# A hybrid decoder step: the RWKV-7 mixer with paired VectorE products, output masks of both head halves at once, and small matmuls on 128 rows

## The chip, the cores and the metric

The kernel runs on one core of a Trainium2 chip. The metric is the device time of one execution in microseconds (us). A core has TensorE (PE, with its weight loads shown apart as PEld), VectorE (DVE), ScalarE (ACT), GpSimd (POOL) and SyncE (SP), which issues most DMAs here. Each engine works through its own instructions in order and waits on semaphores for the others.

## The reference, cut to what matters

One inference step of two layers: layer 0 is a Conformer convolution, layer 1 is RWKV-7 time mixing, and each is followed by a squared-ReLU MLP (1024 → 4096 → 1024). There is one prompt of 1024 tokens behind 16 meta tokens, and 8 samples of one token. Everything is float32. The change lies in layer 1's mixer (16 heads of 64):

```python
def _wkv7_step(S, inp):
    r_t, w_t, k_t, v_t, kk_t, a_t = inp
    sa = jnp.einsum('bhvk,bhk->bhv', S, -kk_t)
    S = (S * w_t[:, :, None, :] + sa[..., None] * (kk_t * a_t)[:, :, None, :]
         + v_t[..., None] * k_t[:, :, None, :])
    y = jnp.einsum('bhvk,bhk->bhv', S, r_t)
    return S, y
...
    r = (xr @ w_r); k = (xk @ w_k); v = (xv @ w_v)
    w_log = -jax.nn.softplus(-(w0 + jnp.tanh(xw @ w1) @ w2)) - 0.5
    decay = jnp.exp(-jnp.exp(w_log))
    a = jax.nn.sigmoid(a0 + (xa @ a1) @ a2)
    g = jax.nn.sigmoid(xg @ g1) @ g2
    kk = k * k_k;  kk = kk / max(|kk| over the head, 1e-12)
    k = k * (1.0 + (a - 1.0) * k_a)
    S_final, ys = lax.scan(_wkv7_step, S0, ...)       # over 1040 tokens
    yn = groupnorm(y per head) * gn_g + gn_b
    out = ((yn + bonus(r, k, v)) * g) @ w_o
```

## The kernel before, in words

A float32 product is made of two half-precise parts, a high and a low one ("hi", "lo", of the type fp32r), and `mm3` (L188 to L190) issues three matmuls for each product: hi·hi, hi·lo, lo·hi. Raw weights come by DMA (`wv_raw`), ACT rounds them to the high part (L158) and DVE or POOL subtracts to get the low part (L163). Activations go the same way (`mx` → `mh`, `ml`, L141 and L142).

The whole step is one function, `hybrid_step`, written as Python generators that are woven into each other; a scheduler then fixes one static order of instructions per engine from its own cost model. Each engine keeps that order. Tiles come from pools with a fixed number of buffers under a tag, so that a tile waits until the last reader of the tile that had its buffer before has finished.

The time runs like this in the profiled execution: layer 0 until about 1105 us; then layer 1's mixers, and behind them the layer-1 MLP until the end. The mixers take the tokens in four groups, g = 0 to 3 (272 columns in group 0: 256 prompt tokens and 16 meta tokens; 256 or 264 in the others). For each group (`mixer_in`) an r loop, a k loop and a v loop run over p = 0 to 7, p being a block of 128 features, two heads. In the k loop, the squares of k are summed per head (`pn`), and `norms` makes the reciprocal norms `r16`, as a hi and a lo part. In the v loop, for each p:

- `l_w` and `l_a` (`lora2`) are the decay's and the rate's low-rank products. Their left sides lie in one tile, `lwah`/`lwal`, w in rows 0 to 63 and a in rows 64 to 127, so that each matmul contracts 64 rows. ACT makes `wa` of both (tanh, then one Copy over both halves).
- `pb` spreads `r16` from heads to features (`spread`, L710), contracting 32 rows.
- DVE makes `kk`, the running sum of the decay (`cum`, by a scan, L1022), `bb` = kk·a, `km`, and four products `ab` (L1050 to L1053) against exponentials `ex` and `em` from ACT.
- `vt` is the transposed v, which ACT copies from PSUM and SP stores to DRAM (`d_v`).

The products go to DRAM in chunks (`d_ab`, `d_v`, `d_p`). A chunk is 64 tokens (chunk 0: 16 meta tokens), and the recurrence runs over chunks 0 to 16 in two generators, `front(c)` and `chunk(c)`. They are woven into the group loops (about ten chunks) and then into the layer-1 MLP (the last ones, until about 2220 us). For each chunk, `front` fetches `xa` and `bk`, multiplies them in four PSUM banks, named `A` (L1131, 128 partitions x 512), and DVE writes them masked (`m_ar`) to `na` and `xa` (L1136, L1137: two operations for each half of the heads, each on 64 partitions x 256). `chunk` makes `gg` from quarters of `na`, builds `p64` as a block-diagonal 128x128 tile (L1177, four operations), then the matmuls `U` (L1210), `S`, and `Y` (L1227 and L1230, the latter on 64 rows and 64 columns).

Of the kernel before, what the change touches and what calls it, by code (L numbers as in the profile page):

```python
# [48 lines left out]
def hybrid_step(tc, x_prompt, x_sample, state_conv, state_shift, state_wkv, meta_tokens,  # L49
# [10 lines left out]
    with ctx:  # L60
# [635 lines left out]
        hspread = masks.tile([P, 2, P], F32R, name="hspread")  # L696
        for o in range(2):
            hs = tt(f"hs{o}", "t2")
            nc.vector.memset(hs[:, :P], 0.0)
            for q in range(2):  # L700
                nc.vector.memset(hs[HALF[q], :P].rearrange("p (i r) -> p i r", r=32)[:, :, 2 * o + q:2 * o + q + 1], 1.0)
# [1 line left out]
            nc.tensor.transpose(pt[:, :P], hs[:, :P], ident)
            nc.scalar.copy(hspread[:, o, :], pt[:, :P])

        def spread(ps, r, p):

            rows = slice(32 * (p // 2), 32 * (p // 2) + 32)
            for i, part in enumerate(r):
                nc.tensor.matmul(ps, hspread[rows, p % 2, :], part[rows], start=i == 0, stop=i == 1,  # L710
                                 tile_position=(rows.start, 0))
# [820 lines left out]
```

## Time and profile before

| | us |
|---|---|
| three runs, median (lowest to highest) | 2965.64 (2964.82 to 2972.77) |
| the profiled execution's own time | 2966.19 |
| its span in the trace | 2964.5 |
| busy: PE / DVE / POOL / ACT | 2767.9 / 2107.8 / 1692.8 / 1351.7 |
| mean granted PE clock | 0.940 |

The profiled execution stands 0.5 us above the median. Times of a view count from the span's start. "Busy" adds up the durations of an engine's instructions; a group's row gives operation, out tile <- in tiles, shapes, count, busy time, mean ns of one, and the idle time of the engine right before with what ended most of it.

### The profile page before, as it was taken

Reading aid. Unit: us, or ns where it says so; the run is one execution under the profiler, and the core shown is the slowest. Engines: PE = TensorE matmul, PEld = TensorE weight load, DVE = VectorE, ACT = ScalarE, POOL = GpSimd, SP = SyncE. Lnnn points to the kernel's source line nnn. Section 1 sums busy time; section 2 is a strip of 40 time slices with the busy share of each in tenths; the row PEclk is TensorE's granted clock in tenths of the full one; section 3 lists DMA queues with packets and bytes.
Section 4 is the critical chain, followed back from the end, with each engine's and each line's share of the span. In section 5 each row is a group of like instructions: output and inputs, shape, how many; then the busy total and the mean of one; then the engine's idle time right before and its main releaser. Section 6 shows DMA issues by size and latency. Waiting matters only on the chain. (4 is left out here: it accounts for less than half of the span.)

```text
span 2964.5 us, 54045 instructions
## 1 busy us (share of the span) xinstructions
PE 2767.9 (93%) x20220; PEld 2611.5 (88%) x20220; DVE 2107.8 (71%) x4126; ACT 1351.7 (46%) x2361; POOL 1692.8 (57%) x2258
## 2 busy tenths in 40 slices
PE   8999999999979997888898888989999999999998
PEld 8998999899979997777787787877889889999998
DVE  5999999974565447779988897798647755344344
ACT  5546444533453434556557657533334553222223
POOL 6677778977887774436334344464337764343342
PEclk9999999999999998887898997988889999999999
DMA  6554444454454435686676866945436642222211
GB/s 179 165 146 130 126 136 135 141 161 141 135 170 139 137 100 154 175 218 178 188 176 165 223 161 172 232 121 144 114 95 219 214 125 90 72 66 70 72 58 40
DMA packets 650044, 421.03 MB, mean 142 GB/s; under 512 B 124752, under 2 KB 604080, under 8 KB 649782
## 3 DMA queue, kind: packets, MB, share of 16 engines
q1 hardware_dynamic: 642436, 414.59, 49.4%
q10 hardware_dynamic: 7122, 2.95, 0.4%
q8 instruction: 159, 2.61, 0.4%
q14 instruction: 103, 0.84, 0.1%
q0 software_dynamic: 224, 0.03, 0.0%
HBM read 347.82 MB, written 70.59 MB: 141 GB/s over the span
## 5 line engine op out<-in xcount | busy, mean ns | idle before, releaser
L163 POOL TENSOR_TENSOR wo_lo<-wo_raw,wo_hi 128x256 fp32r<-128x256 f32 x736 | 557.6, 791 | 348.7 <-ACT wo_hi L158 314.6
L163 POOL TENSOR_TENSOR wi_lo<-wi_raw,wi_hi 128x256 fp32r<-128x256 f32 x640 | 487.9, 795 | 279.6 <-ACT wi_hi L158 274.3
L188 PE MATMUL out<-hh,wo_hi 128*128 128x352 f32 (+2 forms) x1536 | 509.9, 332 | 23.5 <-ACT hh L141 14.0
L320 DVE TENSOR_TENSOR h<-h,out 128x352 f32<-128x352 f32 (+2 forms) x768 | 384.4, 509 | 204.5 <-PE out L190 203.7
L188 PE MATMUL ps_in<-m_h,wi_hi 128*128 128x352 f32 (+2 forms) x1536 | 500.3, 326 | 3.8 <-ACT m_h L247 3.8
L189 PE MATMUL out<-hh,wo_lo 128*128 128x352 f32 (+2 forms) x1536 | 503.6, 328 | 0.0
L190 PE MATMUL ps_in<-m_l,wi_hi 128*128 128x352 f32 (+2 forms) x1536 | 498.1, 325 | 3.7 <-DVE m_l L248 3.6
L189 PE MATMUL ps_in<-m_h,wi_lo 128*128 128x352 f32 (+2 forms) x1536 | 500.6, 326 | 0.0
L190 PE MATMUL out<-hl,wo_hi 128*128 128x352 f32 (+2 forms) x1536 | 496.5, 327 | 3.0 <-DVE hl L142 3.0
L483 DVE SCALAR_TENSOR_TENSOR cv<-u,wdw,cv 128x348 f32<-128x348 f32 (+2 forms) x720 | 377.3, 572 | 0.8
L158 ACT CAST wo_hi<-wo_raw 128x1024 fp32r<-128x1024 f32 x184 | 192.9, 1050 | 366.5 <-PE out L190 176.9
L158 ACT CAST wi_hi<-wi_raw 128x1024 fp32r<-128x1024 f32 x160 | 168.0, 1050 | 407.6 <-PE out L190 208.9
L188 PEld LDWEIGHTS out<-hh,wo_hi 128*128 128x128 f32 x1536 | 296.4, 193 | 31.7 <-ACT hh L141 16.0
L188 PEld LDWEIGHTS ps_in<-m_h,wi_hi 128*128 128x128 f32 x1536 | 292.4, 190 | 7.5 <-ACT m_h L247 4.0
L189 PEld LDWEIGHTS out<-hh,wo_lo 128*128 128x128 f32 x1536 | 295.7, 192 | 2.9
L190 PEld LDWEIGHTS out<-hl,wo_hi 128*128 128x128 f32 x1536 | 292.9, 192 | 5.5 <-DVE hl L142 4.0
L190 PEld LDWEIGHTS ps_in<-m_l,wi_hi 128*128 128x128 f32 x1536 | 291.0, 190 | 7.6 <-DVE m_l L248 4.8
L189 PEld LDWEIGHTS ps_in<-m_h,wi_lo 128*128 128x128 f32 x1536 | 291.3, 190 | 3.3 <-issue 0.2
L307 DVE SCALAR_TENSOR_TENSOR r<-ps_in,rs_m 128x352 f32<-128x352 f32 (+2 forms) x192 | 98.3, 515 | 259.0 <-PE ps_in L190 250.4
L142 POOL TENSOR_TENSOR ml<-mx,mh 128x256 fp32r<-128x256 f32 (+2 forms) x120 | 116.2, 975 | 180.6 <-ACT mh L141 124.2
L142 DVE TENSOR_TENSOR hl<-s,hh 128x352 fp32r<-128x352 f32 (+2 forms) x192 | 136.5, 712 | 104.2 <-ACT hh L141 103.9
L309 ACT ACTIVATE s<-r 128x352 f32<-128x352 f32 (+2 forms) x192 | 93.6, 490 | 142.3 <-DVE r L307 140.9
(398 smaller groups left out, 6404.6 us busy)
## 6 DMA issues: line engine op xcount, KB each, us to landing
wi_raw<-in_w_mlp_in_dram SPq DMA_DIRECT2D x160, 512.0 KB
wo_raw<-in_w_mlp_out_dram SPq DMA_DIRECT2D x160, 512.0 KB
wr_raw<-in_rwkv_w_r_dram SPq DMA_DIRECT2D x32, 512.0 KB
wk_raw<-in_rwkv_w_k_dram SPq DMA_DIRECT2D x32, 512.0 KB
wv_raw<-in_rwkv_w_v_dram SPq DMA_DIRECT2D x32, 512.0 KB
d_ab<-ab SPq DMA_DIRECT2D x32, 512.0 KB
pg_raw<-in_conv_w_pw_dram SPq DMA_DIRECT2D x24, 512.0 KB
pa_raw<-in_conv_w_pw_dram SPq DMA_DIRECT2D x24, 512.0 KB
```

The lines of the kernel that those rows point to most:

```text
L142: eng_lo.tensor_sub(lo, src, hi.bitcast(F32))
L158: nc.scalar.copy(hi[:, :a * b], raw[:, :a * b])
L163: eng_lo.tensor_sub(lo[:, cs], raw[:, cs], hi[:, cs].bitcast(F32))
L188: nc.tensor.matmul(ps, w[0], act[0], start=first, stop=False)
L189: nc.tensor.matmul(ps, w[1], act[0], start=False, stop=False)
L190: nc.tensor.matmul(ps, w[0], act[1], start=False, stop=last)
L307: nc.vector.scalar_tensor_tensor(r[:, :n], ps[:, :n], 0.0, rs[:, :n], op0=ALU.max, op1=ALU.mult)
L309: nc.scalar.activation(s[:, :n], r[:, :n], AF.Square)
L320: nc.vector.tensor_add(hv[:, 4 * i + m, :], hv[:, 4 * i + m, :], ps[:, :n])
L483: nc.vector.scalar_tensor_tensor(acc[m][:, :n], ug[:, m, j:j + n], wdw[:, m, j:j + 1], acc[m][:, :n], op0=ALU.mult, op1=ALU.add)
```

## The change

It touches layer 1's mixer and the norm behind it (`norm_gate`), no loop bounds, and no matmul of the big projections. By count of issued instructions DVE goes from 4128 to 3975, ACT from 2392 to 2563, PE from 17558 to 17692, POOL from 2260 to 2265, and SP stays at 1178. Part by part:

- A banks: `na` is split. `no` (32 of the columns, which only `gg` reads) is written by ACT, unmasked; `nr` is written by DVE for all 128 partitions at once (128x2x64); `xa`'s masked half shrinks from 64x256 to 64x2x64. `xa` becomes two standing tiles, whose zero part is written once.
- `p64` holds two 64-row blocks in place of one 128x128 block: two operations in place of four, and `U` becomes two 64x64 matmuls for each p. `Y`'s second half contracts 128 rows in place of 64.
- `l_w`, `l_a`: each left side has its own 128-row tile (`lwh`, `lwl`, `lah`, `lal`) with zeros in the other half. `pb` contracts 128 rows with a new `hspread`, made by one cast; the two transposes `pth` that made it before are gone.
- The v loop: −kk and k lie side by side, −a and `am` too, so that `bb` and `km` are one product of 128x2xn, and the four `ab` products are two of 128x4x2x64. ACT's one Copy over `wa` becomes one for each half, the decay's first.
- `norms` moves from the v loop's first turn to the end of the k loop.
- In group 0 the 16 meta rows of the transposed v get a tile of their own, `vm`, under the tag of `vt` (one buffer).
- `hmean` is gone; `em` and `ev` take `hsum`, and 1/64 goes into the operations behind them. `wdw` moves to another pool.

```diff
@@ l_w/l_a and spread
+        hspread = masks.tile([P, KT, 2, HS], F32R, name="hspread")
+        nc.vector.tensor_copy(hspread.rearrange("p k q i -> p (k q) i"), ident[:, :2 * KT].unsqueeze(2).broadcast_to([P, 2 * KT, HS]))
...
-                nc.tensor.matmul(ps, hspread[rows, p % 2, :], part[rows], start=i == 0, stop=i == 1,
-                                 tile_position=(rows.start, 0))
+                nc.tensor.matmul(ps, hspread[:, p].rearrange("p q i -> p (q i)"), part, start=i == 0, stop=i == 1)
...
+        lwa = [[lorap.tile([P, N1], F32R, name=f"l{b}{q}") for q in "hl"] for b in "wa"]
...
-                mm3(ps[:, :n], (w[0][rows, p, :], w[1][rows, p, :]), (act[0][rows, :n], act[1][rows, :n]), True, True)
+                mm3(ps[:, :n], (w[0][:, p, :], w[1][:, p, :]), (act[0][:, :n], act[1][:, :n]), True, True)
@@ the end of the k loop
+            norms()
@@ the v loop
-                    vt = pr.tile([P, 3, P], F32, name=nm("vt", p), tag="vt")
+                    vt = pr.tile([P, 2, P], F32, name=nm("vt", p), tag="vt")
...
                     if g == 0:
-                        nc.scalar.copy(vt[:META, 2], pv_[:META, 2 * P:3 * P])
-                        nc.sync.dma_start(d_v[:META, fs_], vt[:META, 2])
+                        vm = pr.tile([P, 2, P], F32, name=nm("vm", p), tag="vt")
+                        nc.scalar.copy(vm[:META, 0], pv_[:META, 2 * P:3 * P])
+                        nc.sync.dma_start(d_v[:META, fs_], vm[:META, 0])
...
-                nc.scalar.activation(wa[:, :, :n], wa[:, :, :n], AF.Copy, scale=0.5, bias=0.5)
+                    nc.scalar.activation(t[:, :n], t[:, :n], AF.Copy, scale=sign, bias=sign)
...
-                nc.vector.tensor_mul(bb[:, :n], kk[:, :n], av[:, :n])
-                nc.vector.tensor_mul(km[:, :n], kp[:, :n], am[:, :n])
+                kb = wa[:, :2, :n]
+                nc.vector.tensor_mul(kb, rk2[:, :2, :n], kb)
...
-                    nc.vector.scalar_tensor_tensor(slots(ab, s, 0), cols(kk, s), -1.0, e(0), op0=ALU.mult, op1=ALU.mult)
-                    nc.vector.tensor_mul(slots(ab, s, 1), cols(rp, s), e(1))
-                    nc.vector.tensor_mul(slots(ab, s, 2), cols(bb, s), cols(em, s))
-                    nc.vector.tensor_mul(slots(ab, s, 3), cols(km, s), cols(em, s))
+                    nc.vector.tensor_mul(out(0), two(rk2[:, 0:3:2, :]), e)
+                    nc.vector.tensor_mul(out(2), two(wa[:, :2, :]), cols(em, s).unsqueeze(2).broadcast_to([P, s[2], 2, s[3]]))
@@ front: the A banks
                 for q in range(2):
-                    r_b, r_k = HALF[q], HALF[1 - q]
-                    nc.vector.tensor_mul(na[r_b, j:j + 2, :], pv[r_b, :, q], mk[r_b])
-                    nc.vector.tensor_mul(xa[r_k, j:j + 2, q, :], pv[r_k, :, q], mk[r_k])
+                    r_k = HALF[1 - q]
+                    nc.scalar.copy(no[Q[2 * q], j:j + 2, :], pv[Q[2 * q], :, q, 32:64])
+                    nc.vector.tensor_mul(xa[r_k, j:j + 2, q, :HS], pv[r_k, :, q, :HS], mk[r_k, :, :HS])
+                    nc.vector.tensor_mul(nr[:, j:j + 2, q, :], pv[:, :, q, HS:], mk[:, :, HS:])
@@ chunk
-            p64 = w_([P, KT, P], "p64", c)
-            for j in range(4):
-                nc.vector.tensor_scalar(p64[:, :, 32 * j:32 * j + 32], p32, in32[:, j:j + 1], None, op0=ALU.mult)
+            p64 = w_([P, KT, HS], "p64", c)
+            for j in range(2):
+                nc.vector.tensor_scalar(p64[:, :, 32 * j:32 * j + 32], p32, par32[:, j:j + 1], None, op0=ALU.mult)
...
-                nc.tensor.matmul(ps[:, p * HS:(p + 1) * HS], p64[:, p, :], w1[:, p, :], start=True, stop=True)
+                for q in range(2):
+                    nc.tensor.matmul(ps[HALF[q], p * HS:(p + 1) * HS], p64[HALF[q], p, :], w1[HALF[q], p, :], start=True, stop=True)
...
-                        nc.tensor.matmul(out(p, q), uv[HALF[q], p, q, :], na[HALF[q], p, HS:], start=False, stop=p == KT - 1)
+                        nc.tensor.matmul(out(p, q), uv[:, p, q, :], nr[:, p, q, :], start=False, stop=p == KT - 1)
```

Lines after the change are one to eleven higher or lower than before (`mm3` stands at L187 to L189). The order of instructions is shown at three places. The rows below give line, operation, out<-in tiles, the out shape, and the semaphores that the instruction waits on, each named after the engine or DMA queue that raises it. An instruction without brackets waits for nothing but its turn.

The first place is ACT's queue in group 0's v loop, around the copies of `vt` of p = 2 while p = 4 is under way. Before:

```order
L962 COPY vt_2_14031<-vt_2_14030 128x256 [waits DMAHW1_49,DMAHW0_49,PE_49]
L965 COPY vt_2_14031<-vt_2_14030 16x128
L1008 ACTIVATE wa_4_14099<-l_w_14100,half 128x272 [waits PE_49]
L1008 ACTIVATE wa_4_14099<-l_a_14105,half 128x272 [waits PE_49]
L1009 ACTIVATE wa_4_14099<-wa_4_14099 128x544 [waits Activation_49]
L1038 ACTIVATE am_4_14200<-wa_4_14099,omka,pvec 128x272 [waits DVE_49,Activation_49]
L1024 ACTIVATE em_4_14192<-wa_4_14099 128x272 [waits DVE_49]
L1028 ACTIVATE ex_4_14194<-wa_4_14099 128x4x64 [waits Pool_49]
L1032 ACTIVATE ex_4_14194<-wa_4_14099 128x16
L1033 COPY wc<-ex_4_14194 128x4 [waits Activation_49]
```

And the same place after the change, from the second tanh on (`vt` of p = 2 is copied two rows ahead of it):

```order
L1009 ACTIVATE wa_4_14064<-l_a_14071,half 128x272 [waits PE_49]
L1010 ACTIVATE wa_4_14064<-wa_4_14064 128x272 [waits Activation_49] x2
L1036 ACTIVATE wa_4_14064<-wa_4_14064,omka,negs 128x272 [waits Activation_49]
L1023 ACTIVATE em_4_14158<-wa_4_14064 128x272 [waits DVE_49]
L1027 ACTIVATE ex_4_14160<-wa_4_14064 128x4x64 [waits Pool_49]
L1031 ACTIVATE ex_4_14160<-wa_4_14064 128x16
L966 COPY vm_2_14010<-vt_2_14003 16x128 [waits DMAHW7_49]
L1032 COPY wc<-ex_4_14160 128x4 [waits Activation_49]
L1034 COPY wc<-ex_4_14160 128x1 [waits Activation_49]
L1014 COPY vv_4_14111<-p_v_14086 128x272 [waits PE_49]
L157 CAST wv_7_hi<-wv_7_raw 128x1024 [waits DMAHW4_49]
L962 COPY vt_3_14117<-vt_3_14116 128x256 [waits DMAHW3_49,PE_49,Activation_49]
```

The copy of the 16 meta rows stood right behind that of the 256 others and waited for nothing; now it stands nine instructions after that copy and waits for a DMA of its own (the store of `vt`, whose buffer it takes), and the next `vt` waits for another (the store of `vm`).

The second place is DVE's queue at two A banks of one chunk (chunk 2). Before:

```order
L1136 TENSOR_TENSOR na_15966<-A_16061,m_ar 64x256 [waits PE_49]
L1137 TENSOR_TENSOR xa_15957<-A_16061,m_ar 64x2x128
L1136 TENSOR_TENSOR na_15966<-A_16061,m_ar 64x256
L1137 TENSOR_TENSOR xa_15957<-A_16061,m_ar 64x2x128
L1136 TENSOR_TENSOR na_15966<-A_16068,m_ar 64x256 [waits PE_49]
L1137 TENSOR_TENSOR xa_15957<-A_16068,m_ar 64x2x128
L1136 TENSOR_TENSOR na_15966<-A_16068,m_ar 64x256
L1137 TENSOR_TENSOR xa_15957<-A_16068,m_ar 64x2x128
```

DVE's queue after the change:

```order
L1142 TENSOR_TENSOR xa_12558<-A_16025,m_ar 64x2x64 [waits Activation_49]
L1143 TENSOR_TENSOR nr_15921<-A_16025,m_ar 128x2x64
L1183 TENSOR_SCALAR p_16360<-p_15923,par32q 128x8x32
L1094 TENSOR_TENSOR tt_20_18114<-ni_17839 128x220 [waits DVE_49]
L1142 TENSOR_TENSOR xa_12558<-A_16034,m_ar 64x2x64 [waits Activation_49]
L1143 TENSOR_TENSOR nr_15921<-A_16034,m_ar 128x2x64
L1142 TENSOR_TENSOR xa_12558<-A_16025,m_ar 64x2x64 [waits Activation_49]
L1143 TENSOR_TENSOR nr_15921<-A_16025,m_ar 128x2x64
```

And ACT's queue after the change at the same two banks (before, ACT had nothing to do there):

```order
L1141 COPY no_15922<-A_16025 32x64 [waits PE_49]
L1219 COPY uv<-U_15990 64x8x64 [waits DVE_49]
L1141 COPY no_15922<-A_16034 32x64 [waits PE_49]
L893 COPY st_6_18079<-p_r_17963 128x256 [waits DMAHW6_49,PE_49,Activation_49]
L1141 COPY no_15922<-A_16025 32x64 [waits DVE_49]
L157 CAST wg_hi<-wg_raw 128x1024 [waits DMAHW2_49]
L140 CAST mh_2_1_18175<-mx_2_1_18173 128x256 [waits PE_49]
L140 CAST mh_2_2_18181<-mx_2_2_18179 128x256 [waits PE_49]
L140 CAST mh_2_3_18187<-mx_2_3_18185 128x256 [waits PE_49]
L1141 COPY no_15922<-A_16034 32x64 [waits DVE_49]
```

DVE waited once for PE at each bank and then worked through it alone; now a bank goes ACT, DVE, ACT, DVE, and each of the 136 `xa` operations of the program waits on ACT.

The third place is PE's queue in group 1's v loop at p = 3. Before:

```order
L188 MATMUL l_w_16598<-lwah_14576,wa_hi 128x256 [waits Activation_49]
L189 MATMUL l_w_16598<-lwah_14576,wa_lo 128x256
L190 MATMUL l_w_16598<-lwal_14577,wa_hi 128x256
L710 MATMUL pb_3_16731<-r16h_16116,hspread 128x256 [waits DVE_49]
L710 MATMUL pb_3_16731<-r16l_16117,hspread 128x256
L188 MATMUL l_a_16603<-lwah_14576,wa_hi 128x256 [waits Activation_49]
L189 MATMUL l_a_16603<-lwah_14576,wa_lo 128x256
L190 MATMUL l_a_16603<-lwal_14577,wa_hi 128x256
```

And after:

```order
L699 MATMUL pb_3_16686<-r16h_16084,hspread 128x256 [waits DVE_49]
L699 MATMUL pb_3_16686<-r16l_16085,hspread 128x256
L974 MATMUL nn_1_16508<-ab_1_16443 32x32 [waits DVE_49,PE_49]
L974 MATMUL nn_1_16508<-ab_1_16443 32x32 x15
L987 MATMUL pk_1_16526<-rk_1_16441,hsum 128x256
L187 MATMUL l_w_16552<-lwh,wa_hi 128x256 [waits Activation_49]
L188 MATMUL l_w_16552<-lwh,wa_lo 128x256
L189 MATMUL l_w_16552<-lwl,wa_hi 128x256
L187 MATMUL l_a_16558<-lah,wa_hi 128x256 [waits Activation_49]
L188 MATMUL l_a_16558<-lah,wa_lo 128x256
L189 MATMUL l_a_16558<-lal,wa_hi 128x256
```

`pb` moves ahead of the products `nn` and `pk` of the p before, and `l_w` and `l_a` stand next to each other, each with its own left side.

More of the change, by code (lines that the diff above doesn't have):

```diff
@@ L688, in hybrid_step @@
         open_tmp(ld, N1, "1", 3, side="right")
-        PB = [32 * (p // 2) + 2 * (p % 2) for p in range(KT)]
+        PB = [2 * p for p in range(KT)]
         hsel = masks.tile([P, PB[-1] + P], F32, name="hsel")
@@ L717, in hybrid_step @@
         ddec = masks.tile([P, KT, 6, DEC], F32, name="ddec")
+        negs = masks.tile([P, 2 * KT], F32, name="negs")
+        for i, b in enumerate(("k_k", "k_a")):
+            nc.vector.tensor_scalar(negs[:, i * KT:(i + 1) * KT], pvec[:, col[b]:col[b] + KT], -1.0, None, op0=ALU.mult)
+        nvec = lambda b, p: negs[:, (b == "k_a") * KT + p:(b == "k_a") * KT + p + 1]
         omka = masks.tile([P, KT], F32, name="omka")
@@ L730, in hybrid_step @@
         open_ep(ld, 2, "d", max(GN[i][1] for i in GN_OF[0]))
+        lwa = [[lorap.tile([P, N1], F32R, name=f"l{b}{q}") for q in "hl"] for b in "wa"]
+        for i in range(2):
+            for t in lwa[i]:
+                nc.scalar.copy(t[HALF[1 - i]], hsel[HALF[1 - i], 0:1].broadcast_to([HS, N1]))
         prep = {}
         VSLOW = 0.5
-        AMB = 1
         PL_K = (1, 2)
@@ L840, in decay_rate @@
                 nc.scalar.copy(lf[64:, :n], ps)
-                split(lwa[0][:, :n], lwa[1][:, :n], lf[:, :n], nc.gpsimd)
+                for rows, (hi, lo) in zip(HALF, lwa):
+                    split(hi[rows, :n], lo[rows, :n], lf[rows, :n], nc.gpsimd)
             def gate():
@@ L1077, in hybrid_step @@
             nc.gpsimd.memset(st["sv"][HALF[q], :, q, :], 0.0)
+        xas = [wk.tile([P, KT, 2, P], F32, name=f"xa{i}") for i in range(2)]
+        for t in xas:
+            for q in range(2):
+                nc.gpsimd.memset(t[HALF[1 - q], :, q, HS:], 0.0)
         def inverses(c, n):
@@ L1141, in front @@
             nc.vector.transpose(flat(x32), flat(p32))
-            chunks[c] = xa, bk, na, p32, x32, vt
+            chunks[c] = xa, bk, nr, no, p32, x32, vt
             yield RW[2]
@@ L1157, in chunk @@
             yield from fronts.setdefault(c, front(c))
-            xa, bk, na, p32, x32, vt = chunks.pop(c)
+            xa, bk, nr, no, p32, x32, vt = chunks.pop(c)
             sv, uv = st["sv"], st["uv"]
@@ L1203, in chunk @@
             for i in (0, 2):
-                nc.scalar.copy(p64[Q[i], :, 32 * i + 32:32 * i + 64], pv[Q[i]])
+                nc.scalar.copy(p64[Q[i], :, 32:64], pv[Q[i]])
             step(c + 1)
@@ L1209, in chunk @@
             for p in range(KT):
[L1210 removed]
+                for q in range(2):
+                    nc.tensor.matmul(ps[HALF[q], p * HS:(p + 1) * HS], p64[HALF[q], p, :], w1[HALF[q], p, :], start=True, stop=True)
             nc.vector.tensor_copy(uv[HALF[0], :, 0, :], kv(ps)[HALF[0]])
@@ L1340, in norm_gate @@
                 ps = bank(f"em{g}{p}", "w")
-                nc.tensor.matmul(ps[:, :n], hmean, y, start=True, stop=True)
-                nc.vector.tensor_sub(y, y, ps[:, :n])
+                nc.tensor.matmul(ps[:, :n], hsum, y, start=True, stop=True)
+                nc.vector.scalar_tensor_tensor(y, ps[:, :n], -1.0 / HS, y, op0=ALU.mult, op1=ALU.add)
                 nc.scalar.activation(sq, y, AF.Square)
@@ L1345, in norm_gate @@
                 ps = bank(f"ev{g}{p}", "w")
-                nc.tensor.matmul(ps[:, :n], hmean, sq, start=True, stop=True)
-                nc.scalar.activation(sq, ps[:, :n], AF.Sqrt, bias=eps_t[:, 2:3])
+                nc.tensor.matmul(ps[:, :n], hsum, sq, start=True, stop=True)
+                nc.scalar.activation(sq, ps[:, :n], AF.Sqrt, scale=1.0 / HS, bias=eps_t[:, 2:3])
                 nc.vector.reciprocal(sq, sq)
```

71 lines of the change are left out of this document (28 added, 43 removed).

## The prediction

> **What bounds the kernel now.** I read the busy times by stage first, then the chain of waits, then the groups by shape of DVE, ACT and PE, and last the time line at the places that change. All times are of the profiled execution (2966.2 us, 0.5 us above the median of the runs). A measurement of this kernel can tell about 0.3%, 9 us, from no change. Busy time by stage; the first three rows hold what changes (mixers from group 0's v loop on, then the MLP with the last chunks in it), the last does not:
>
> ```profile
> core 0: us, PE busy (x) PEld busy (x) DVE busy (x) ACT busy (x) POOL busy (x), PEclk, DMA share, GB/s
> 1250.00:1890.00 640.00, 562.07 (x5834) 492.15 (x5833) 564.97 (x1222) 398.47 (x844) 264.40 (x361) 0.88 0.71 185
> 1890.00:2050.00 160.00, 141.82 (x1203) 120.97 (x1202) 125.06 (x265) 59.04 (x104) 91.53 (x103) 0.83 0.68 164
> 2050.00:2220.00 170.00, 169.65 (x1439) 140.00 (x1439) 108.68 (x230) 53.68 (x89) 67.66 (x86) 0.90 0.43 107
> 2220.00:2964.00 744.00, 722.85 (x4488) 710.72 (x4486) 384.98 (x662) 258.17 (x418) 351.20 (x463) 0.99 0.33 103
> ```
>
> In the mixers PE and DVE are both 88% busy (562 and 565 of 640 us), ACT 62%. Neither alone is the bound: they pass work back and forth. From 2050 us on PE is full. The chain that ended last, kept from 1654 us, shows the passing in its shares for 1654 to 1890, with two pieces of the last chunks behind it:
>
> ```profile
> by line: PE A L1131 5.4%; issue 5.1%; DVE mx L776 3.5%; DVE na L1136 2.9%; DVE xa L1137 2.8%; ACT L1347 2.7%; DMA bk<-d_ab 2.7%; PE p_r L188 2.4%; PE p_r L190 2.4%; PE p_v L188 2.2%; PE p_r L189 2.2%; PE bT L1188 2.1%; ACT L1008 1.9%; PE p_
> ...
> 2123.20 2.16 DVE p L1177 x4
> 2165.51 1.28 PE U L1210 x12
> ```
>
> No line has more than 5.4%. The two DVE lines that the change shortens most (L1136, L1137) have 5.7% of 236 us, 13.5 us. So a microsecond off DVE buys part of one: I take a third, because DVE is near full but PE is as near.
>
> **DVE's part.** The groups that go, and the rows that price what comes:
>
> ```profile
> L1137 DVE TENSOR_TENSOR xa<-A,m_ar 64x256 f32<-64x256 f32 x136 | 57.4, 422 | 2.5
> L1136 DVE TENSOR_TENSOR na<-A,m_ar 64x256 f32<-64x256 f32 x136 | 56.4, 415 | 12.8 <-PE A L1131 12.4
> L1177 DVE TENSOR_SCALAR p<-p,in32q 128x256 f32<-128x256 f32 x68 | 27.0, 453 | 0.0
> L1052 DVE TENSOR_TENSOR ab<-bb,em 128x256 f32<-128x256 f32 x32 | 16.5, 516 | 0.0
> L1050 DVE SCALAR_TENSOR_TENSOR ab<-kk,ex 128x256 f32<-128x256 f32 x32 | 15.0, 469 | 0.0
> L1237 DVE TENSOR_TENSOR fs<-S,wc 128x512 f32<-128x512 f32 x17 | 11.6, 681 | 2.2 <-PE S L1219 2.1
> L1040 DVE TENSOR_TENSOR bb<-kk,wa 128x256 f32<-128x256 f32 x16 | 9.9, 620 | 0.1
> L1042 DVE TENSOR_TENSOR km<-rk,am 128x256 f32<-128x256 f32 x16 | 8.1, 506 | 0.0
> L975 DVE TENSOR_TENSOR n<-nn,nmask 128x128 f32<-128x128 f32 x32 | 8.8, 274 | 4.0 <-PE nn L973 2.5 <-PE nm L981 1.5
> ```
>
> Masks: 272 operations of 256 elements a partition stay 272 but have 128. The 128-element read of PSUM in this trace takes 274 ns (`n`), so 272 x 0.274 = 74.5 us replace 113.8: −39 us of busy DVE. On the path: the 13.5 us of the chain shrink by 35%, 4.7 us in 236, hence −13 in 640 us, and −2 after 1890: **−15**.
>
> `p64`: 34 of 68 go, 34 x 0.453 = −15 us busy; in the piece of four, 2.16 us, half goes. I take a quarter of the busy time: **−4**.
>
> Pairs: `ab` takes four operations for each p, two by `ex` and two by `em`, of about 0.49 (the mean of the two rows; 1.95 us); two of 512 elements at 0.681 (`fs`, the nearest of that length) make 1.36, −0.6. `bb` and `km` (1.13) become one of about 0.68, −0.45; but if a product of 512 elements runs at the four-operation rate (2 x 0.49) nothing is won. Bounds −34 and 0 busy for 32 p; I take −22 and, at a little over a quarter, **−6** on the path.
>
> **ACT's new part in the masks.** ACT gets 136 copies `no` of 32x64, each between two DVE operations, as the order above shows. Nothing in the trace is that hand-over; the nearest are copies on ACT and DVE's waits for ACT:
>
> ```profile
> L1173 ACT COPY gg<-gg 32x256 f32<-32x256 f32 x34 | 12.4, 365 | 12.7 <-PE gg L1165 12.2
> L1033 ACT COPY wc<-ex 128x4 f32<-128x4 f32 x32 | 6.3, 197 | 0.2
> DVE wa L1022 <- ACT wa L1009: 10.3, 10, 1.8
> DVE wk_lo L163 <- ACT wk_hi L158: 0.6, 2, 0.5
> ```
>
> A copy of 64 elements lies between 0.197 (4 elements) and 0.365 (256): some 0.22, 30 us of busy ACT, which goes to 67% in the mixers and so hides most of it. The waits are another matter: ACT takes its copies in order behind casts and evictions, and the A bank (one of PE's four) comes free later. The scan's 10.3 us over the 24 p of that stretch are 0.43 each, `wk_lo`'s 0.6 us over its 24 operations 0.03. So 136 hand-overs cost between 4 and 58 us of idle DVE. I take 0.15 each, nearer the low end because DVE has other work queued between the banks (the second place of the order): 20 us idle, and at the same third and a bit for banks held longer, **+8**. Behind a waiting `no` on ACT stand `uv`, a weight cast and activation casts, and PE waits for those.
>
> The one Copy over `wa` becomes two; the first is half as long, so that the scan's 10.3 us of waiting shrink, and ACT pays a second overhead of about 0.1 in 32 places. Both are near 3 us: **0**.
>
> **PE's small matmuls.** Durations overlap here, so I go by starts:
>
> ```profile
> 1856.10 0.39 PE L188 MATMUL l_a<-lwah,wa_hi 64*128 64x264 f32 x1
> ...
> 1856.66 0.39 PE L188 MATMUL p_v<-mh,wv_hi 128*128 128x264 f32 x1
> 1856.88 0.28 PE L189 MATMUL p_v<-mh,wv_lo 128*128 128x264 f32 x1
> 1857.00 0.28 PE L190 MATMUL p_v<-ml,wv_hi 128*128 128x264 f32 x1
> ...
> 1867.70 0.28 PE L710 MATMUL pb<-r16l,hspread 32*128 32x264 f32 x1
> 1867.91 0.39 PE L188 MATMUL l_w<-lwah,wa_hi 64*128 64x264 f32 x1
> 1867.92 0.39 PE L188 MATMUL l_a<-lwah,wa_hi 64*128 64x264 f32 x1
> ...
> 1868.48 0.70 PE L1131 MATMUL A<-xa,bk 128*128 128x256 f32 x2
> ```
>
> A lone product of three 64-row matmuls takes 0.56 (1856.10 to 1856.66), and `p_v`'s first one on 128 rows another 0.22 where the next steps by 0.12. So going from one row count to another costs 0.1 a time. Where `l_w` and `l_a` stand together, both run at once, 0.57 for six (1867.91 to 1868.48). On 128 rows six take 6 x 0.12 = 0.72. The 32 pairs thus gain 2 x 0.56 − 0.72 = 0.40 each if they ran alone, and lose 0.15 if they ran at once: −13 to +5 us, and I take −4. `pb`, 0.21 a matmul (1867.70 to 1867.91) by 64, can go to 0.12: −6. `U` (0.107 a step in the chain's piece) goes to twice as many 64x64 ones, and `Y`'s 64-row half to 128 rows:
>
> ```profile
> L703 PE MATMUL pth<-ident,hs 128*128 128x128 f32 x2 | 0.7, 373 | 3.3 <-DVE hs L701 3.3
> 1862.26 1.15 PE L1230 MATMUL Y<-na,uv 64*64 64x64 f32 x32
> ```
>
> `Y` steps by 0.036 (1.15 for 32); two of that kind in place of one `U` are 0.07 for 0.107, −10 over 272, and nothing if they wait for their weights; `Y` stays. I take −4. PE's sum is −14 busy; by its part in the mixers' chain (no line holds more than 5.4%, all its lines less than half) **−6**. Without `pth` the 3.3 us that PE stood for `hs` go, at a point where the weights wait too: **−3**, and 0 at worst.
>
> The Trainium skill has a rule that speaks against this part: "TensorE: Matmul & The Clock Gate", Part 3 (packing small matmuls), says that matmuls on few rows in different row groups run at once, and that one on 32 rows takes as long as one on 128. The two `l` at 1867.91 agree with the first half. By it alone I estimate 0.55 us lost for each of the pairs that ran at once, some 9 us, and PE's term would be +2 in place of −6, the end 2958.
>
> **norms** moves ahead of the first v projection. What it can save is the wait of the first `pb`, and what it can cost is the same, on the k loop's last products:
>
> ```profile
> L710 PE MATMUL pb<-r16h,hspread 32*128 32x272 f32 x8 | 3.5, 438 | 5.1 <-DVE kk L1020 4.9 <-ACT r16h L141 0.2
> ```
>
> 5.1 us are idle in group 0, most of them for `kk`, which norms feeds; over four groups between −10 and +5: **−2**. The DVE and POOL operations on zeros, `hmean` and `wdw` are done once, beside a full PE in layer 0 and 1: 0.
>
> **Group 0's vm.** Copy and store of `vt` were one pair; now they are a ring with one buffer:
>
> ```profile
> 1253.91 0.38 ACT L962 COPY vt<-vt 128x256 f32<-128x256 f32 x1
> 1254.18 0.25 ACT L965 COPY vt<-vt 16x128 f32<-16x128 f32 x1
> ...
> 1259.73 0.37 ACT L962 COPY vt<-vt 128x256 f32<-128x256 f32 x1
> ...
> 1255.78 0.62 SPq L963 DMA_DIRECT2D d_v<-vt  x1
> 1256.49 0.41 SPq L966 DMA_DIRECT2D d_v<-vt  x1
> ...
> 1798.11 1.65 DMA d_z<-ey
> 2328.85 4.96 DMA d_z<-ey
> ```
>
> A p takes about 5.8 us (1253.91 to 1259.73). Its ring now is: copy 0.38, 1.6 us until SP issues (1254.18 to 1255.78), the store, copy 0.25, issue 0.4, the second store. A store to DRAM takes 1.65 to 4.96 (the two `d_z`). Short stores give 0.4 + 1.6 + 1.65 + 0.25 + 0.4 + 1.65 = 6.0 us, as long as a p, so nothing; long ones 12.6, which over 8 p is +54 if each p waits it out. But the wait stands eight places behind in ACT's queue, so the ring only binds where it is longer than a p: with stores near 3 us it is 8.7, 2.9 over, +22. I take half, **+12**. Behind the waiting copy on ACT stand `wc`, `vv` and a weight cast; on SP, in order, the store of `vm` holds up `rk2`'s fetch and `d_ab`.
>
> **Sum.** −15 − 4 − 6 + 8 + 0 − 6 − 3 − 2 + 12 = −16: 2966.2 − 16 = **2950 us**, likely range 2932 to 2964.
>
> **Rivals.** *Lock-step at the A bank (slower).* ACT's `no` of the second half waits for DVE, and DVE's next `xa` for it. If ACT comes each time behind one cast or eviction, a hand-over costs some 0.4 (the scan's 0.43): 54 us of idle DVE. DVE's saving of 39 + 15 + 22 = 76 counts a third, −25; idle in the middle of a bank also holds the bank from PE, so I count half, +27 in place of +8: the end is 2969, and 2978 at 0.55 each. From 0.3 us a wait it eats the rest of the gain. For it speaks that ACT shows 62% busy and never had this work; against it, that ten waits for ACT's `wa` cost only 10.3 us in 640.
> *DVE is the bound after all.* Then the 76 us less the 20 of idle count fully in 640 of 800 us, with the other terms about −45 to −60: 2905 to 2920. For it: 88% busy; against: 5.7% of the chain.
> *Nothing comes of it.* PE's projections and weight transfers (DMA share 0.71) set the mixers' pace, small gains are eaten by `vm`: 2957 to 2975. For it: PE is equally full.
> *Vm's ring binds fully* (+22 to +54): 2960 to 2975.
> *The rule above on rows holds*: 2958.
>
> **How the numbers follow.** Forecast 0.40; lock-step 0.16; DVE the bound 0.14; nothing 0.16; the ring 0.09; the rule on rows 0.05. Faster by over 9 us (under 2957): 0.36 of the forecast, 0.14 of the second, and of the rest 0.05, 0.55. Slower (over 2975): 0.13 of lock-step, 0.03 of the ring, 0.04 of nothing and the forecast, 0.20. Between: 0.25. The range leaves out a tenth on each side: 2912 (DVE the bound, upper half) to 2982 (lock-step at 0.55 and the ring).
>
> **What would show it.** Masks: `xa` and `nr` near 274 ns. `p64` 34 times. Pairs: two `ab` operations near 0.68. Hand-overs: DVE's waits for ACT at `xa`, near 20 us; 54 means lock-step. Group 0: ACT's waits for `d_v`, near 12. PE: `l`, `pb` on 128 rows at steps of 0.12. The stage 1250 to 1890 should lose some 12 us, the later two 4, and the last none. It goes wrong if masks of 64 or 128 partitions stay near 0.4 (a fixed cost), or if the weights' transfers take up what DVE gives.

## The result, and the profile after

The changed kernel takes 2948.81 us (median of six runs, 2946.08 to 2955.22) against 2967.1 before (2964.82 to 2972.77): a ratio of 0.9938, 95% interval 0.9924 to 0.9952, some 18 us less. Among the further kernels below, one execution of u_vm and one of m_y64 were slow (3343 and 3674 us at granted clocks of 0.74 and 0.66), and the ratios leave them out. The profiled execution of the changed kernel took 2951.4 us, with a span of 2949.4 and a mean granted clock of 0.948. The forecast was 2950.

The place, however, is another than forecast. This is the busy time by stage of the changed kernel, in the same windows as before:

```profile
core 0: us, PE busy (x) PEld busy (x) DVE busy (x) ACT busy (x) POOL busy (x), PEclk, DMA share, GB/s
1250.00:1890.00 640.00, 541.77 (x6000) 480.31 (x5999) 525.71 (x1100) 411.04 (x956) 264.11 (x364) 0.90 0.71 183
1890.00:2050.00 160.00, 124.28 (x1242) 106.58 (x1242) 118.45 (x261) 64.79 (x125) 81.19 (x100) 0.85 0.67 172
2050.00:2220.00 170.00, 170.00 (x1634) 144.72 (x1633) 110.53 (x246) 69.60 (x136) 85.56 (x109) 0.97 0.53 143
2220.00:2964.00 744.00, 707.51 (x4366) 695.63 (x4364) 371.45 (x638) 250.32 (x403) 337.88 (x444) 0.98 0.31 95
```

In the mixers DVE is 39 us less busy (565 to 526) and PE 20 (562 to 542). Fixed windows don't tell whether that time was won, so one looks for the same instruction in both time lines. The mixers' last projection, before and after:

```profile
1885.80 0.29 PE L190 MATMUL p_v<-ml,wv_hi 128*128 128x264 f32 x1
```

```profile
1886.60 0.28 PE L189 MATMUL p_v<-ml,wv_hi 128*128 128x264 f32 x1
```

And the last `Y` of the recurrence, before and after:

```profile
2213.50 1.15 PE L1230 MATMUL Y<-na,uv 64*64 64x64 f32 x32
```

```profile
2195.63 1.11 PE L1236 MATMUL Y<-nr,uv 128*64 128x64 f32 x32
```

The mixers end where they ended. Everything is won in the 328 us behind them, which I call the tail: the last seven chunks beside the layer-1 MLP. (Behind the last `Y`, 3 us are lost again.) Its windows, from the last `p_v` to the last `Y`, before and then after:

```profile
1886.20:2214.60 328.40, 309.87 (x2666) 259.84 (x2665) 234.52 (x499) 113.27 (x192) 161.80 (x193) 0.86 0.56 136
```

```profile
1887.00:2196.70 309.70, 273.98 (x2761) 231.94 (x2760) 214.67 (x484) 122.98 (x245) 151.98 (x192) 0.91 0.58 148
```

PE issues more instructions after, yet is busy 36 us less, and its granted clock is 0.91 in place of 0.86. The MLP's own matmuls, which the change does not touch, are shorter there. Groups by shape in the tail, before:

```profile
L188 PE MATMUL ps_in<-m_h,wi_hi 128*128 128x328 f32 x125 | 46.3, 371 | 3.8 <-ACT m_h L247 3.8
L188 PE MATMUL out<-hh,wo_hi 128*128 128x328 f32 x96 | 36.7, 382 | 0.0
```

And after:

```profile
L187 PE MATMUL ps_in<-m_h,wi_hi 128*128 128x328 f32 x127 | 44.4, 351 | 5.2 <-ACT m_h L246 5.2
L187 PE MATMUL out<-hh,wo_hi 128*128 128x328 f32 x96 | 33.3, 347 | 0.8 <-ACT hh L140 0.8
```

Two things in the time line of before make them long. A big matmul that stands alone between pairs of small ones makes a round of 0.60 us with its pair (2131.81 to 2132.41, two steps of some 0.3), at a granted clock of 1.00, where a big one in a row steps by 0.15 (2124.55 to 2124.70) and 32 `Y` in a row take 1.15 us. And the clock falls to 0.50 behind such a stretch. PE's time line, and the granted clock (the third number from the end) by stretches of 2 and 4 us:

```profile
2124.55 0.31 PE L188 MATMUL ps_in<-m_h,wi_hi 128*128 128x328 f32 x1
2124.70 0.31 PE L189 MATMUL ps_in<-m_h,wi_lo 128*128 128x328 f32 x1
...
2131.81 0.41 PE L188 MATMUL ps_in<-m_h,wi_hi 128*128 128x328 f32 x1
2132.16 0.32 PE L1230 MATMUL Y<-na,uv 64*64 64x64 f32 x2
2132.41 0.41 PE L189 MATMUL ps_in<-m_h,wi_lo 128*128 128x328 f32 x1
2132.76 0.32 PE L1230 MATMUL Y<-na,uv 64*64 64x64 f32 x2
...
2141.16 0.47 PE L188 MATMUL ps_in<-m_h,wi_hi 128*128 128x328 f32 x1
2141.43 0.47 PE L189 MATMUL ps_in<-m_h,wi_lo 128*128 128x328 f32 x1
```

```profile
2124.00:2128.00 4.00, 4.00 (x57) 3.77 (x56) 3.94 (x10) 0.00 (x0) 0.95 (x2) 1.00 0.54 154
2132.00:2134.00 2.00, 2.00 (x11) 1.17 (x10) 1.91 (x5) 0.54 (x1) 1.89 (x2) 1.00 0.28 82
2136.00:2140.00 4.00, 4.00 (x48) 3.04 (x43) 0.47 (x1) 2.52 (x6) 3.32 (x5) 0.50 0.44 54
2140.00:2144.00 4.00, 4.00 (x16) 3.84 (x16) 0.04 (x1) 0.59 (x1) 0.00 (x0) 0.50 0.33 66
```

Counted over the records of the tail, 108 of the 855 matmuls of `mm3` stand alone between small ones before, and 65 of 860 after. From start to next start all of them take 179 and 159 us, and those that stand alone 41 and 24: 18 of the 20 us. The trace's clock record, which holds only 1.00 and 0.50 here, has 89 us at 0.50 in the tail before and 58 after; if that halves the pace, the 31 us are worth some 15 (an estimate, and partly the same time as the 18). So most of the gain is time of the MLP's matmuls, by the order that they stand in and the clock that they are granted.

The operations themselves came out near their prices. DVE's groups by shape (1105 to 2220 us), after:

```profile
L1142 DVE TENSOR_TENSOR xa<-A,m_ar 64x128 f32<-64x128 f32 x136 | 38.7, 285 | 24.8 <-ACT no L1141 22.9
L1143 DVE TENSOR_TENSOR nr<-A,m_ar 128x128 f32<-128x128 f32 x136 | 38.2, 281 | 1.0
L1052 DVE TENSOR_TENSOR ab<-wa,em 128x512 f32<-128x512 f32 x32 | 26.3, 823 | 0.0
L1051 DVE TENSOR_TENSOR ab<-rk,ex 128x512 f32<-128x512 f32 x32 | 25.9, 809 | 3.7 <-issue 2.7 <-ACT ex L1027 0.9
L1039 DVE TENSOR_TENSOR wa<-rk,wa 128x512 f32<-128x512 f32 x16 | 14.4, 901 | 2.0 <-ACT wa L1036 2.0
L1183 DVE TENSOR_SCALAR p<-p,par32q 128x256 f32<-128x256 f32 x34 | 11.0, 354 | 0.0
```

ACT's group of the copies, and ACT's waits in group 0's v loop:

```profile
L1141 ACT COPY no<-A 32x64 f32<-32x64 f32 x136 | 27.2, 201 | 101.0 <-PE A L1135 50.2 <-DVE nr L1143 36.2 <-DMA zr<-d_z 12.6
```

```profile
ACT vm L966 <- DMA d_v<-vt: 6.2, 3, 3.0
ACT vt L962 <- DMA d_v<-vm: 3.5, 3, 1.5
```

### The profile page after: what moved, and what is told of

It reads as the page before. It is cut to its first block, busy times and chain, and to the rows that moved or that the text cites. A ratio compares the mean times of both kernels' runs of the same rounds, so it can differ in the third digit from the quotient of the medians.

```text
span 2949.4 us, 54588 instructions
## 1 busy us (share of the span) xinstructions
PE 2712.2 (92%) x20490; PEld 2573.4 (87%) x20490; DVE 2049.2 (69%) x3973; ACT 1379.4 (47%) x2532; POOL 1688.3 (57%) x2263
## 5 line engine op out<-in xcount | busy, mean ns | idle before, releaser
L187 PE MATMUL out<-hh,wo_hi 128*128 128x352 f32 (+2 forms) x1536 | 509.6, 332 | 27.2 <-ACT hh L140 17.9
L187 PE MATMUL ps_in<-m_h,wi_hi 128*128 128x352 f32 (+2 forms) x1536 | 497.7, 324 | 5.2 <-ACT m_h L246 5.2
L189 PE MATMUL ps_in<-m_l,wi_hi 128*128 128x352 f32 (+2 forms) x1536 | 498.3, 325 | 2.3 <-DVE m_l L247 2.2
L189 PE MATMUL out<-hl,wo_hi 128*128 128x352 f32 (+2 forms) x1536 | 493.8, 325 | 2.2 <-DVE hl L141 2.2
L187 PEld LDWEIGHTS out<-hh,wo_hi 128*128 128x128 f32 x1536 | 295.5, 192 | 35.6 <-ACT hh L140 20.7
L187 PEld LDWEIGHTS ps_in<-m_h,wi_hi 128*128 128x128 f32 x1536 | 291.3, 190 | 7.6 <-ACT m_h L246 5.4
L189 PEld LDWEIGHTS ps_in<-m_l,wi_hi 128*128 128x128 f32 x1536 | 289.9, 189 | 6.2 <-DVE m_l L247 3.6
L189 PEld LDWEIGHTS out<-hl,wo_hi 128*128 128x128 f32 x1536 | 291.3, 190 | 4.3 <-DVE hl L141 3.0
```

The lines of the kernel that those rows point to most:

```text
L187: nc.tensor.matmul(ps, w[0], act[0], start=first, stop=False)
L189: nc.tensor.matmul(ps, w[0], act[1], start=False, stop=last)
```

## The experiments

All ratios are to the kernel before, run beside each on its chip; "last `p_v`" and the tail are read in each kernel's profile as above.

| kernel | ratio (95%) | last `p_v` | tail us | PE busy in it | clock |
|---|---|---|---|---|---|
| before | 1 | 1886 | 328 | 310 | 0.86 |
| changed | 0.9938 (0.9924–0.9952) | 1887 | 310 | 274 | 0.91 |
| u_masks | 0.9981 (0.9965–0.9998) | 1887 | 331 | 308 | 0.86 |
| b_masks | 0.9919 (0.9893–0.9945) | 1899 | 303 | 275 | 0.90 |
| b_u64 | 0.9958 (0.9939–0.9976) | 1872 | 332 | 308 | 0.88 |
| y64 | 0.9855 (0.9824–0.9887) | 1870 | 305 | 277 | 0.90 |
| u_vm | 0.9889 (0.9866–0.9913) | 1873 | 312 | 280 | 0.91 |
| u_rows | 0.9889 (0.9863–0.9915) | 1887 | 300 | 273 | 0.91 |
| u_pairs | 0.9935 (0.9910–0.9959) | 1879 | 320 | 288 | 0.88 |
| m_y64 | 0.9970 (0.9959–0.9982) | 1879 | 322 | 291 | 0.88 |
| no_dve | 0.9964 (0.9951–0.9978) | 1894 | 308 | 274 | 0.91 |
| b_order | 0.9983 (0.9966–1.0000) | 1878 | 337 | 313 | 0.87 |
| a_order | 0.9828 (0.9809–0.9848) | 1869 | 295 | 277 | 0.92 |
| best1 | 0.9903 (0.9883–0.9922) | 1885 | 312 | 284 | 0.90 |

**u_masks**: the masks' part undone, with `Y`'s second half on 64 rows again.

```diff
-                    nc.scalar.copy(no[Q[2 * q], j:j + 2, :], pv[Q[2 * q], :, q, 32:64])
-                    nc.vector.tensor_mul(xa[r_k, j:j + 2, q, :HS], pv[r_k, :, q, :HS], mk[r_k, :, :HS])
-                    nc.vector.tensor_mul(nr[:, j:j + 2, q, :], pv[:, :, q, HS:], mk[:, :, HS:])
+                    nc.vector.tensor_mul(na[r_b, j:j + 2, :], pv[r_b, :, q], mk[r_b])
+                    nc.vector.tensor_mul(xa[r_k, j:j + 2, q, :], pv[r_k, :, q], mk[r_k])
```

> The changed kernel with the A banks' masks and Y as they were before (na and xa by DVE, Y's second half on 64 rows, no copies on ACT); all else changed. In the two traces the mixers end at the same time (last p_v at 1886 before, 1887 after), and the whole gain lies behind, between there and the last Y (2214 before, 2196 after), where the granted clock is 0.97 in 2050 to 2220 us after and 0.90 before. Theory A (PE in the last chunks: Y on 128 rows keeps the clock up and saves switches): most of the 18 us are lost, 2960 to 2967, and the clock there falls to about 0.90. Theory B (the prediction's: masks are -15 and +8, mostly in the mixers): 2956. Theory C (the scheduler's new order alone): 2949, clock as after.

Measured 0.9981: two thirds of the gain are gone, and the tail is back, in length, busy time and clock:

```profile
1887.00:2218.00 331.00, 307.67 (x2723) 253.68 (x2720) 221.84 (x472) 111.95 (x190) 156.24 (x193) 0.86 0.55 136
```

**b_masks**: the reverse, this part alone put into the kernel before (the diff above read backwards, and `wdw` in its new pool).

> The kernel before with the masks' part alone: nr for both halves on DVE, no on ACT, Y on 128 rows (and wdw in the other pool, for room). Theory A: 2950 to 2955, with the clock of 2050 to 2220 at 0.95 or more. Theory B: -15 + 8 = -7, 2959. Lock-step between ACT and DVE: 2967 or more. Theory C: anything within 5 of 2966.

Measured 0.9919, 24 us faster, at least as much as the whole change (the two intervals overlap). The tail is the short one, though the mixers end 13 us later than before:

```profile
1899.50:2202.50 303.00, 275.45 (x2617) 239.41 (x2615) 214.97 (x486) 122.22 (x240) 152.08 (x190) 0.90 0.59 149
```

So theories B (masks worth 7 us, mostly in the mixers) and C (any new order would do) fall for the tail, and lock-step falls altogether.

**b_u64**: `p64` and `U` alone put into the kernel before.

```diff
-            for j in range(4):
-                nc.vector.tensor_scalar(p64[:, :, 32 * j:32 * j + 32], p32, in32[:, j:j + 1], None, op0=ALU.mult)
+            for j in range(2):
+                nc.vector.tensor_scalar(p64[:, :, 32 * j:32 * j + 32], p32, par32[:, j:j + 1], None, op0=ALU.mult)
```

> The kernel before with p64's and U's part alone (two DVE operations in place of four, two 64x64 matmuls in place of one 128x128). Theory B: p64 -4 and a part of PE's -6 : 2959 to 2962. Theory A with activity counted by rows and columns in use: U on quarter tiles lowers the clock, so no more than -3: 2963 to 2967. The wait for p64 as the cause of the tail: 2952 to 2958.

Measured 0.9958, 12 us faster, with the tail as long as before (332) and the mixers' end 14 us earlier. It does not shorten the tail.

**y64**: the changed kernel with `Y`'s second half on 64 rows, v's part of y left out.

```diff
-                        nc.tensor.matmul(out(p, q), uv[:, p, q, :], nr[:, p, q, :], start=False, stop=p == KT - 1)
+                        nc.tensor.matmul(out(p, q), uv[HALF[q], p, q, :], nr[HALF[q], p, q, :], start=False, stop=p == KT - 1)
```

> The changed kernel with Y's second half on 64 rows again (each matmul takes only the 64 rows of its own head half, so that v's part of y is left out); same count of matmuls, DVE and ACT unchanged. Theory A by Y's rows: the clock in 2050 to 2220 falls from 0.97 to about 0.90 and the time goes to 2956 to 2964. If DVE's shorter masks or fewer waits make the tail: 2949 within 3.

Measured 0.9855, and the clock did not fall: `Y`'s 128 rows are not what keeps it up, so that part of theory A is refuted. That it is 25 us faster than the changed kernel was foreseen by no theory. From start to next start the 512 `Y` of this half take 28.0 us here and 28.1 there, 0.055 each (the expectation's 0.053 is not there). What differs is the order of instructions from 1514 us on, between group 1's v loop and group 2's, since the scheduler plans anew for every edit.

**u_vm**: the 16 meta rows back in `vt`'s tile.

```diff
-                        vm = pr.tile([P, 2, P], F32, name=nm("vm", p), tag="vt")
-                        nc.scalar.copy(vm[:META, 0], pv_[:META, 2 * P:3 * P])
+                        nc.scalar.copy(vt[:META, 2], pv_[:META, 2 * P:3 * P])
```

> The changed kernel with group 0's 16 meta rows of v back in vt's tile (no ring of copy, store, copy, store). Prediction: the ring costs 12, so the time is the changed kernel's 2949 less 12, on a chip where before takes 2967 (ratio about 0.990), with the gain in the v loop of group 0 (its last p_v 1289 in the changed kernel). Rival, order alone: in the changed kernel's trace ACT waits 6.2 us for the store of vt and 3.5 for that of vm in all, so no more than 5 us, and any larger move comes from another order behind group 0.

Measured 0.9889, 0.49% less than the changed kernel or 14.5 us, with 8 us of uncertainty by the two intervals, and all of it is in the mixers (the tail is 312 us). Its last projection:

```profile
1873.38 0.29 PE L189 MATMUL p_v<-ml,wv_hi 128*128 128x264 f32 x1
```

The prediction's 12 lie within that. Of ACT's waits of 6.2 + 3.5 us for the two stores, one of 2.6 for `vt`'s is left:

```profile
ACT vt L962 <- DMA d_v<-vt: 2.6, 1, 2.6
```

By group 1's v loop (1377 against 1385) 8 us are won, 2 of them by the end of group 0's (1287.0 against 1288.9); the rest comes later and may be order. The other kernels bear the 8 out: from group 0's first `p_v` to group 1's first it takes 167 to 172 us in the seven that have the ring (changed, u_masks, y64, u_rows, u_pairs, m_y64, no_dve), and 159 to 161 in the three that are the changed kernel without it (u_vm, a_order, best1).

**u_rows**: `l_w`, `l_a` on 64 and `pb` on 32 rows again, with `pth`'s two transposes.

```diff
-                mm3(ps[:, :n], (w[0][:, p, :], w[1][:, p, :]), (act[0][:, :n], act[1][:, :n]), True, True)
+                mm3(ps[:, :n], (w[0][rows, p, :], w[1][rows, p, :]), (act[0][rows, :n], act[1][rows, :n]), True, True)
```

> The changed kernel with l_w and l_a on 64 rows and pb on 32 rows again (and pth's two transposes). Prediction: these were worth about -8, so 2957 (ratio 0.997). The rule of few rows running at once: faster by up to 9, 2940 (ratio 0.991). In the changed kernel's trace l and pb step by 0.2 us in the mixers as they did before, so the theory formed after it says: within 4 of the changed kernel unless the order moves.

Measured 0.9889, 14.5 us faster than the changed kernel, so the predicted gain of 8 from more rows is not there. But the gain is not these matmuls' either: the mixers, where they run, end at 1887.19, and the 10 us by which the tail is shorter lie where none of them runs:

```profile
1887.40:2187.10 299.70, 273.04 (x2781) 231.98 (x2779) 212.28 (x483) 123.30 (x245) 150.78 (x189) 0.91 0.59 148
```

**u_pairs**: the paired products as single ones.

```diff
-                nc.vector.tensor_mul(kb, rk2[:, :2, :n], kb)
+                for i in range(2):
+                    nc.vector.tensor_mul(kb[:, i], rk2[:, i, :n], kb[:, i])
```

(and the two `ab` products as four).

> The changed kernel with the paired products undone (bb, km and the four ab products as six operations of their own, all else as changed). Prediction: pairs were worth 6, 2955 (ratio 0.996). In the trace two paired ab operations take 0.81 and 0.82 us against about 0.49 each for four, -0.3 us a p, so busy DVE rises by about 17 us, and if DVE were the bound of the mixers by that much: 2966.

Measured 0.9935, 1 us from the changed kernel: the pairs bring nothing that can be told, with some 8 us of uncertainty by the two intervals, and the order moved too (the mixers end 7 us earlier, the tail is 11 longer). DVE as the bound (2966) is out.

**m_y64**: `Y` on 64 rows, in full (its own line changed as in y64).

```diff
-                    nc.vector.tensor_mul(xa[r_k, j:j + 2, q, :HS], pv[r_k, :, q, :HS], mk[r_k, :, :HS])
-                    nc.vector.tensor_mul(nr[:, j:j + 2, q, :], pv[:, :, q, HS:], mk[:, :, HS:])
+                    nc.vector.tensor_mul(xa[r_k, j:j + 2, q, :], pv[r_k, :, q], mk[r_k])
+                    nc.vector.tensor_mul(nr[HALF[q], j:j + 2, q, :], pv[HALF[q], :, q, HS:], mk[HALF[q], :, HS:])
```

> The changed kernel with Y's second half on 64 rows, done in full: xa's masked half is 64x256 again (it holds v's part of y), nr only the own half's 64x128, no by ACT as changed. DVE gains 136 x about 0.14 = 19 us. The y64 kernel was 0.8% faster than the changed one though a Y matmul steps by 0.053 us there and 0.055 in the changed kernel. If 64 rows are what makes it faster: 2935 or less (ratio 0.989). If it was the order: anywhere from 2940 to 2960, and the tail behind the mixers (about 305 to 310 us with the clock at 0.97) stays, since the masks' part with ACT stays.

Measured 0.9970, slower than any expectation but the order's upper end. The tail is 322 us at a clock of 0.88, where 305 to 310 was expected: with `xa`'s longer masks two thirds of its gain are lost.

**no_dve**: the copies `no` on DVE.

```diff
-                    nc.scalar.copy(no[Q[2 * q], j:j + 2, :], pv[Q[2 * q], :, q, 32:64])
+                    nc.vector.tensor_copy(no[Q[2 * q], j:j + 2, :], pv[Q[2 * q], :, q, 32:64])
```

> The changed kernel with the copies no on DVE in place of ACT: DVE works a bank through alone, no hand-over; it gains 136 copies of 32x64 of about 0.2, 27 us, ACT loses 30. Prediction (hand-overs cost +8 on the path, DVE counts a third): -8 + 9, 2950, ratio 0.994. If the hand-overs were the cost of the mixers, as in the rival lock-step: 2930, 0.988. Of the tail (309.9 us from the last p_v to the last Y in the changed kernel, 328.6 before): if shorter DVE work at a bank is what shortens it, DVE has here 1.12 + 0.4 us a bank against 1.68 before, so 318 to 325; if taking ACT in is what matters: 325 or more; if neither: 310.

Measured 0.9964, 8 us slower than the changed kernel, and the mixers end 7 us later (1894). The tail stays short at 308 us. So nothing shows that the hand-overs to ACT cost time in the mixers, and ACT's part is not what shortens the tail either. DVE has 1.57 us of work a bank here, more than in m_y64 (1.41), whose tail is 14 us longer; that speaks against my line by DVE's work a bank.

**b_order**: the same operations as before, in another order.

```diff
-        RW = [4.0, 2.4, 3.12, 5.0, 5.0, 1.28, 3.12, 0.8, 3.0]
+        RW = [4.0, 2.4, 3.12, 4.9, 4.9, 1.28, 3.12, 1.0, 3.0]
```

> The kernel before, the same operations, with three of the nine costs that place a chunk's steps among the other work moved (5.0, 5.0, 0.8 to 4.9, 4.9, 1.0), so that only the order differs from the middle of the mixers on. If order alone moves the time by no more than a measurement can tell: within 5 of before. If order alone is worth as much as the parts (u_rows moved the tail by 10 us, y64 the mixers by 17, without a cheaper operation there): 10 to 20 either way, with the tail still above 320 and the clock about 0.90, if the masks' part is what shortens the tail.

Measured 0.9983: the sum moved by 5 us (the interval reaches 1), but out of two larger moves, the mixers 8 us shorter and the tail 9 longer.

**a_order**: the same line changed in u_vm.

> u_vm (the changed kernel without vm's ring) with the same three costs moved, so only the order differs from u_vm's ratio of 0.9889. Within 5 us of it if order does not matter; 10 to 20 either way if it does, the tail staying near 310 and the clock at 0.95 or more.

Measured 0.9828, 18 us faster than u_vm by order alone (9 us of uncertainty by the two intervals), and 51 faster than before: the fastest of all, faster than both kernels. The tail is 295 us at much the same busy time (277 against 280), so PE waits less there:

```profile
1869.30:2164.00 294.70, 276.88 (x2737) 233.59 (x2735) 207.95 (x476) 122.93 (x242) 154.24 (x190) 0.92 0.60 152
```

**best1**: u_vm and u_rows together (both diffs above).

> The changed kernel without vm's ring and with l, a and pb on 64 and 32 rows: the two parts undone that were faster one by one (0.9889 each, against 0.9938). If both gains are the operations' own they add up: 0.984, 2919 on the first chip. If u_rows' gain was its order (its mixers ended with the changed kernel's, 1887, and its tail was 10 shorter, where none of its operations run): between 0.984 and 0.992, most likely about 0.989.

Measured 0.9903, no faster than either alone (the intervals overlap) and 19 us short of the sum: the gains don't add up. Neither u_vm's early end of the mixers (1885 here, 1873 there) nor u_rows' short tail (312 against 300) is there, so u_rows' gain, and what u_vm won behind the ring's 8 us, look like order and not like the operations' own.

What holds through all of this is one thing. Four kernels have the old masks (before, u_masks, b_u64, b_order): tails of 328 to 337 us, PE busy 308 to 313. Ten have the new, m_y64 only in part: 295 to 322 us, busy 273 to 291. The two sets don't overlap in spite of the reordering, though each tail is read from one profiled execution and the gap between the sets is 6 us. Two pairs (changed and u_masks, before and b_masks) differ in this part alone but for `wdw`'s pool in the second, by 21 and 25 us, where order alone moved a tail by 9 (b_order) and 18 (a_order). So that the masks' part shortens the tail is shown.

How it does is not. What is left is that the scheduler, with this part, puts fewer big matmuls alone between small ones (64 to 89 in the ten kernels, 99 to 112 in the four, by my count). The clock goes along with it. By the clock records it fell to 0.50 behind 3.4 us without idle time on PE 6 or 7 times in the tails of the four, 2 to 4 times in nine of the ten, and 6 times in m_y64. And the tails come, by groups, in the order of the time that they spend at 0.50: 44 us in the shortest (295), 51 to 65 in those of 300 to 312, 75 and 79 in those of 320 and 322, 82 to 96 in those of 328 to 337. An experiment that keeps the old masks and forces the other order was not made, so order as the link is argued, not shown.

## Why the prediction was right, and where it was not

The time, the range and the sign held, and the likeliest case was the right one by its sum (−16 against −18). By place it was wrong: it put −12 into the mixers and −4 behind them, and measured were +1 and −19. Two errors cancelled, so that the sum came out is luck. By its steps:

- **Masks, DVE's part (−15, of it −13 in the mixers).** The price by the 274 ns row was right: 285 and 281 ns, busy time down 37 us where 39 were said. The step that failed is the one that turned it into time, the share of the chain from 1654 to 1890 drawn out over the mixers: put in alone (b_masks), this part made the mixers' end 13 us later and the tail 25 shorter; taken out (u_masks), it left the mixers' end where it was and made the tail 21 longer. So the −13 is in neither pair, though order moves that end by as much (17 us in y64), and the tail, put at −2, got it all. DVE was as busy as PE, but the mixers' end did not move with its 39 us.
- **Hand-overs (+8 on the path, 20 us idle).** Idle ahead of `xa` is 22.9 us for ACT, in 20 waits of which one is 11.7; the old wait for PE there (12.4) is gone. The idle time was priced right as a total, but not as 0.15 at each hand-over: 116 of the 136 show no wait. The +8 on the path is not seen: moving the copy to DVE made it 8 us slower. The lock-step rival is refuted: 22.9 us is 0.17 a hand-over, against the 0.4 that it needed.
- **`p64` (−4) and `U`.** An operation takes 354 ns now, 0.1 us less than was counted, and `U`'s busy time went from 36.3 to 27.4 us, near the −10 counted. Alone the two gave −12 (interval −7 to −18), about the −4 and all of PE's −6; part of it may be order.
- **Pairs (−6).** Mis-sized: 0.81 and 0.82 us an operation, not the 0.681 of the nearest row, hence −0.32 us a p for `ab`, and 0.90 for `bb` with `km`, −0.22. That is 17 us of busy DVE in place of 22, and on the path nothing that can be told from the 8 us of uncertainty, in which the −6 lies too.
- **`l`, `pb` and `pth` on PE (part of −6, and −3).** Not there: the kernel without them is faster. At a granted clock of 1.00, `l_w` and `l_a` step by a median of 0.125 us, as counted, but `pb` by 0.21, where 0.12 was counted (0.225 before), so its −6 of busy time was mis-sized. The rule of the Trainium skill that the prediction cited against this part gave 8 us more than my sum. u_rows moved that rule's way, but where none of these matmuls runs, so it is neither shown nor refuted here.
- **norms (−2)** was not tried alone. The wait that it was to shorten did not shrink: PE's idle time ahead of `pb` is 9.7 us before and 17.9 after, over all its rows.
- **`vm` (+12).** Right in sign and near in size: the ring costs some 8 us by group 1's v loop (six other kernels with the ring and two without agree), more of it behind group 0's v loop than in it. The rest of u_vm's 14.5 us may be order.
- **What the sum had no term for.** An order that changes with every edit is worth up to 18 us (a_order), as much as the whole change; and the clock of the stage from 2050 to 2220 us, which I quoted at 0.90 and took as given, rose to 0.97.

## What to carry to other kernels

Check a right sum by place: find the same instruction in both time lines, since two wrong terms can add up to the right time. Where a scheduler plans the order anew, run the same operations with a slightly different plan before you credit a part with its few us; here order alone was worth up to 18 us (a_order against u_vm), and the effects of parts did not add. Where small matmuls are mixed into large ones, count the large ones that stand alone and look at the granted clock: that, more than busy VectorE, was where this kernel's tail had time to lose, and a_order, which also lacks vm's ring, shows that some 30 us more are to be had.
